# A list-scheduled opening for the first feed-forward stage of a decoder layer

## The chip, the cores and the metric

The kernel runs on one core of a Trainium2 chip. The metric is the device time of one execution in microseconds (us); the median of three runs is given. Five engines matter: TensorE (PE, matmuls; PEld is its weight load), VectorE (DVE), ScalarE (ACT), GpSimd (POOL) and SyncE (SP), which issues the DMAs.

## The reference

One decoder layer on 1,040 tokens (16 meta tokens and 1,024 of the sequence), width 1,024: a half-step SwiGLU, a mix of sparse and sliding-window attention, a second half-step SwiGLU, a last norm. What the change touches is the first SwiGLU:

```python
h = h + 0.5 * swiglu(rmsnorm(h, norm_ffn1[l]), w_ffn1_gate[l], w_ffn1_up[l], w_ffn1_down[l])

def rmsnorm(x, g):
    xf = x.astype(jnp.float32)
    y = xf * lax.rsqrt(jnp.mean(xf * xf, axis=-1, keepdims=True) + EPS)
    return (y * g.astype(jnp.float32)).astype(x.dtype)

def swiglu(x, w_gate, w_up, w_down):
    return (jax.nn.silu(x @ w_gate) * (x @ w_up)) @ w_down
```

with d_ff = 2816, all in float32. The attention stage between the two feed-forward stages is left as it is in code; the way in which it is ordered is touched (below).

## The kernel before

**Data.** Activations stand transposed: eight tiles `h[x][k]` of 128 features each, for two token halves x = 0 (528 columns, meta tokens among them) and x = 1 (512). A float32 operand is split into a high and a low float16 part; a product is three float16 matmuls (high by high, high by low, low by high, `mm3`, L438). Splitting is one ScalarE copy (high) and one VectorE subtraction (low): `split_w` (L421) for weights, `split_x` (L528) for activations.

**Feed-forward stage** (`ffn`, L521). The 22 blocks of d_ff go in pairs. From the second part on, a pair's gate or up weights are multiplied by a seven-product form of a 2 by 2 block product (`fast`, L711): combined weights (`sums`, L627) meet combined activation blocks t1 to t4 (tiles `tb`), and VectorE adds the seven results up as they leave the product banks pa, pb, pc and pd (`half_products`, L742, order `UP`, L730). Each such job is 168 matmuls, and while it runs the steps of the next job's weights (`prepare`, L672) and the splits of the finished hidden blocks (`split_later`, L831) are dealt out between its products by `pump` (L702).

**The opening.** The loads are issued in the order h[0], the identity, the gains, two weights, h[1]. The norm of half 0 (`norm_stats`, L460, `norm_bcast`, L478, `norm_u`, L502) squares on ScalarE and sums on VectorE; that of half 1 squares and sums on GpSimd (L927 to L931). `norm_stats` corrects the reciprocal root with four small VectorE steps. The first pair is multiplied plainly (`plain_pair`, L562): all of half 0 for gate, then `other_half()` (norm of half 1), then up, and half 1 after that. Before half 1's products the first combined weights (`wide_weights`, L650) and the combined blocks (`make_t`, L593) are ordered: twelve normed tiles are computed anew in float32 (`gained`, tiles `tu`), combined by four subtractions per block on GpSimd (`combine`, L584) and split. The normed tiles are not kept, but for four of half 1 (`saved`). All this runs in the order in which it is written.

**The planner.** The attention stage, with the last passes of the feed-forward stage ahead of it, isn't run as written: `Plan` (L136) records the instructions (`add`, L185), and `run` (L220) orders them by a list schedule with a cost for each (`cost`, L153). It takes, at each step, the engine that can go first and, there, the ready instruction recorded earliest. A tile in a product bank counts as one whole in its dependences (L83), a buffer is free when its last-recorded user is done (L242), and a VectorE instruction with two float32 inputs outside the banks is priced 0.4 us higher while GpSimd works (L214, L292). Each engine then runs its instructions in the order so found.

Of the kernel before, what the change touches and what calls it, by code (L numbers as in the profile page):

```python
# [46 lines left out]
class View:  # L47
# [34 lines left out]
    def box(self):  # L82
        if self.base.whole or not self.ops or not isinstance(self.ops[0], tuple):  # L83
            return None
        idx = self.ops[0][1]
        idx = [i for i in (idx if isinstance(idx, tuple) else (idx,)) if i is not None]
        res = []
        for i, n in zip(idx, self.base.shape):
            if isinstance(i, int):
                res.append((i % n, i % n + 1))  # L90
            elif isinstance(i, slice) and (i.step in (None, 1)):
                a, b, _ = i.indices(n)
                res.append((a, b))
            else:
                res.append((0, n))
        return res
# [9 lines left out]
class Lazy(View):  # L106
    def __init__(self, shape, dt, make, key, bufs, whole):
        View.__init__(self, self, (), shape, dt)
        self.make, self.key, self.bufs, self.whole = make, key, bufs, whole
        self.made = None  # L110
        self.live = False
        self.seen = []
        self.last = self.first = None
# [22 lines left out]
class Plan:  # L136
# [48 lines left out]
    def add(self, engine, op, args, kw):  # L185
# [34 lines left out]
    def run(self, keep=(), margin=0.25, early=0.0):  # L220
# [21 lines left out]
        for b in tiles.values():  # L242
            if id(b) not in kept and b.last is not None:
                dies[b.last].append(b)
# [30 lines left out]
        while len(order) < count:  # L275
# [51 lines left out]
        for b in tiles.values():  # L327
            b.seen, b.first, b.last = [], None, None
# [17 lines left out]
def layer_kernel(ctx: ExitStack, tc: tile.TileContext, xT, gains, wgu1, wd1, win, wvi, wbs, wbw, wout,  # L346
# [53 lines left out]
    ph["S"] = 2  # L400

    h = [[hp([P, HW[x]], F32, "h") for _ in range(KD)] for x in range(2)]

    def load_h(x):
        for k in range(KD):
            nc.sync.dma_start(h[x][k], xT[k][:, HS0[x]:HS0[x + 1]])

    load_h(0)
    ident = new(cst, [P, P], F32, name="ident")
    nc.sync.dma_start(ident, eye)  # L410
    g_all = new(cst, [P, 4, KD], F32, name="g_all")
    nc.sync.dma_start(g_all, gains)
# [47 lines left out]
    def norm_stats(acc, subs):  # L460
# [60 lines left out]
    def ffn(u, rb, hs, gi, wgu, wd, other_half, passes, saved, before_passes):  # L521
# [40 lines left out]
        def plain_pair(f):  # L562
            ws = [load_w(wgu[2 * f + i], 1024, raws.pop(0) if raws else None) for i in range(4)]
# [147 lines left out]
        def fast(weights, blocks, order):  # L711
# [5 lines left out]
                    "p53": ("pd", s4, b22, wb, wb, False)}  # L717
# [24 lines left out]
        def half_products(m, blocks, first, done):  # L742
            make = fbtmp if m else ftmp
            for what, ps in joint(blocks, UP):
# [17 lines left out]
                else:  # L762
                    c12 = va(base)[:, :, :wb]
                    nc.vector.tensor_add(c12, ps, c12)
                    done(1, base, c12)

# [72 lines left out]
        vals = plain_pair(0)  # L839
        blocks = (u[0][:4], u[0][4:], u[1][4:]) + tuple(t_blocks)  # L840
        with tc.manual_schedule(engines=ORDERED):
            for f0, f1 in F_GROUPS:
# [4 lines left out]
                for f in range(f0, f1, 2):  # L847
# [16 lines left out]
                    if f < NF - 2:  # L864
                        gates = gate_part(blocks)
# [46 lines left out]
    u1, rb1 = [], []  # L912

    def ffn1_norm(x):
        acc = new_acc() if x == 0 else acc_b
        for k in range(KD if x == 0 else 0):
            square_into(k, h[x][k], acc)
        u, rb = norm_u(norm_stats(acc, SUB_ALL[x]), h[x], 0, SUB_ALL[x], keep=True, saved=saved1 if x else None)
        u1.append(u)
        rb1.append(rb)  # L920

    saved1 = {}
    raws = [load_raw(wgu1[i], 1024) for i in range(2)]
    load_h(1)
    ffn1_norm(0)
    acc_b = new_acc()
    for k in range(KD):  # L927
        sq = acc_b if k == 0 else ftmp("sq")
        nc.gpsimd.tensor_mul(sq[:, :512], h[1][k], h[1][k])
        if k:  # L930
            nc.gpsimd.tensor_add(acc_b[:, :512], acc_b[:, :512], sq[:, :512])  # L931
# [8 lines left out]
    def to_mix():  # L940
# [4 lines left out]
    acc = ffn(u1, rb1, h, 0, wgu1, wd1, lambda: ffn1_norm(1),  # L945
              ((0, SUB_ALL[0], lambda r: mix_norm(0, r)), (1, SUB_ALL[1], None)), saved1, to_mix)
# [596 lines left out]
```

## Time and profile before

| | us |
|---|---|
| median of three runs | 2007.55 |
| lowest and highest | 2007.20, 2009.01 |
| the profiled execution, its own time | 2009.06 |
| its span, first to last instruction | 2007.3 |
| TensorE busy in the span | 1922.9 |
| VectorE busy | 1630.3 |
| ScalarE busy | 898.2 |
| GpSimd busy | 385.1 |

The first feed-forward stage takes up to about 640 us, the attention stage to about 1350, the second feed-forward stage the rest. Busy time is an average over stages with different limits; what one stage is worth is read from that stage. Neighbouring instructions of one engine can overlap a little, so that the distance between their starts is shorter than their durations.

### The profile page before, as it was taken

What the parts mean: (1) busy time and instruction counts of PE and PEld (TensorE: products, weight loads), DVE (VectorE), ACT (ScalarE), POOL (GpSimd) and SP (SyncE); (2) the same over time, 40 slices, a digit from 0 to 9 for tenths busy, and PEclk for the clock granted to TensorE, in tenths of its full rate; (3) what the DMA queues carried; (4) which work ended last, traced back from release to release, by engine and by line L of the source; (5) the groups of instructions that cost most, each with busy time, mean ns of one, the idle gap of its engine ahead of it and who ended that gap; (6) DMA issues with size and microseconds to landing.
All of it is one profiled execution on the core that took longest, in us unless ns stands there. A gap on an engine that the chain in (4) does not pass through costs nothing.

```text
span 2007.3 us, 32840 instructions
## 1 busy us (share of the span) xinstructions
PE 1922.9 (96%) x13080; PEld 1201.4 (60%) x13080; DVE 1630.3 (81%) x2787; ACT 898.2 (45%) x1602; POOL 385.1 (19%) x313
## 2 busy tenths in 40 slices
PE   5899999999998999999999999998899999999997
PEld 4588888888887655655555656444344444444443
DVE  7988778788774899999998977566987888788767
ACT  4434233333322455669887555434333333243232
POOL 4511312221220033131000000002322213312200
PEclk9899999999999999999999999999999999999998
DMA  4011111211121554221111231341112111211213
GB/s 160 11 54 58 59 64 38 69 64 59 48 85 38 190 160 149 69 91 64 32 48 43 85 102 52 105 147 42 43 38 68 63 58 48 64 63 48 79 37 131
DMA packets 58873, 146.95 MB, mean 73 GB/s; under 512 B 7264, under 2 KB 13408, under 8 KB 58720
## 3 DMA queue, kind: packets, MB, share of 16 engines
q1 hardware_dynamic: 58720, 144.86, 22.6%
q8 instruction: 102, 1.67, 0.3%
q14 instruction: 51, 0.42, 0.1%
HBM read 130.01 MB, written 14.76 MB: 72 GB/s over the span
## 4 chain that ended last, share of the span: by engine, by line
PE 79%; DVE 12%; ACT 5%; issue 2%; DMA 1%; POOL 1%; SPq 0%; DVEq 0%; ACTq 0%; POOLq 0%
PE pc L188 15%; PE pd L188 15%; PE pa L188 15%; PE pb L188 7%; PE p_gate L326 7%; PE p_out L326 4%; PE p_br L326 3%; PE pdn L188 2%; PE ptr L326 2%; PE rp L326 2%; ACT jk L326 1%; PE pdn L326 1%; PE pv_b L326 1%; DVE wsp L326 1%; DVE sc L326 1%
## 5 line engine op out<-in xcount | busy, mean ns | idle before, releaser
L188 PEld LDWEIGHTS <-wsp 128*128 128x128 f16 x4848 | 478.0, 99 | 293.2 <-issue 30.9
L188 PEld LDWEIGHTS <-x 128*128 128x128 f16 x3132 | 307.2, 98 | 156.5 <-issue 7.0
L326 PEld LDWEIGHTS <-wsp 128*128 128x128 f16 x2448 | 235.8, 99 | 223.0 <-issue 6.9
L188 PE MATMUL pa<-u,wsp 128*128 128x264 f16 (+1 forms) x1440 | 224.7, 310 | 0.0
L326 PE MATMUL p_gate<-u,wsp 128*128 128x512 f16 x768 | 188.4, 379 | 0.0
L188 POOL TENSOR_TENSOR h<-h,base 128x512 f32<-128x512 f32 (+1 forms) x72 | 116.3, 1615 | 291.1 <-DVE base L188 229.7
L326 PE MATMUL rp<-u,wsp 128*128 128x512 f16 (+2 forms) x624 | 140.2, 366 | 4.0 <-DVE rt L326 3.7
L188 ACT ACTIVATE wsp<-wst 128x1024 f16<-128x1024 f32 (+2 forms) x88 | 80.4, 915 | 142.3 <-DMA wst<-in_wd_dram 50.4
L326 DVE SCALAR_TENSOR_TENSOR wsp<-wst,wsp 128x1024 f16<-128x1024 f32 (+2 forms) x104 | 107.5, 1036 | 27.3 <-ACT wsp L326 27.0
L188 PE MATMUL pb<-tb,wsp 128*128 128x264 f16 (+1 forms) x720 | 114.0, 312 | 8.7 <-ACT tb L188 5.9
L188 PE MATMUL pc<-tb,x 128*128 128x264 f16 (+1 forms) x720 | 114.0, 313 | 5.1 <-DVE c L188 5.0
L326 ACT ACTIVATE wsp<-wst 128x1024 f16<-128x1024 f32 (+2 forms) x104 | 91.1, 880 | 58.4 <-PE p_out L326 16.4
L188 PE MATMUL pc<-tb,wsp 128*128 128x256 f16 (+1 forms) x720 | 113.6, 313 | 0.0
L188 PE MATMUL pd<-u,x 128*128 128x256 f16 (+1 forms) x720 | 110.7, 308 | 0.0
L188 PE MATMUL pd<-tb,x 128*128 128x256 f16 (+1 forms) x720 | 110.7, 308 | 0.0
L188 POOL TENSOR_TENSOR t<-g,g 128x512 f32<-128x512 f32 x16 | 25.5, 1592 | 434.4 <-DVE g L188 434.4
L188 ACT ACTIVATE wsp<-sa 128x1024 f16<-128x1024 f32 (+1 forms) x64 | 62.3, 973 | 101.4 <-DVE sa L188 101.2
L326 ACT ACTIVATE jk<-sc,s5nb 128x784 f16<-128x784 f32 (+2 forms) x93 | 98.1, 1055 | 15.9 <-DVE s5nb L326 13.1
L188 PE MATMUL pa<-hid,wsp 128*128 128x264 f16 (+1 forms) x648 | 103.1, 310 | 0.0
L188 PE MATMUL pd<-hid,x 128*128 128x256 f16 (+1 forms) x648 | 101.6, 308 | 0.0
L188 DVE TENSOR_TENSOR c<-pc,base 128x512 f32<-128x512 f32 x80 | 55.4, 692 | 55.1 <-PE pc L188 54.8
L188 ACT ACTIVATE base<-pa 128x528 f32<-128x528 f32 (+1 forms) x64 | 38.2, 598 | 133.6 <-PE pa L188 133.6
(218 smaller groups left out, 3494.7 us busy)
## 6 DMA issues: line engine op xcount, KB each, us to landing
wst<-in_wgu_dram SPq DMA_DIRECT2D x88, 512.0 KB, 3.8
wst<-in_win_dram SPq DMA_DIRECT2D x44, 512.0 KB, 3.5
wst<-in_wd_dram SPq DMA_DIRECT2D x48, 384.0 KB, 3.5
wst<-in_wd_dram SPq DMA_DIRECT2D x32, 256.0 KB, 2.8
wst<-in_wout_dram SPq DMA_DIRECT2D x16, 512.0 KB, 3.7
qscr<-ry SPq DMA_DIRECT2D x20, 256.0 KB, 2.1
q<-qscr SPq DMA_DIRECT2D x20, 256.0 KB, 3.1
wst<-in_wbs_dram SPq DMA_DIRECT2D x16, 256.0 KB, 3.2
```

The source lines that it names most:

```text
L188: return getattr(engine.real, op)(*[give(a) for a in args], **{k: give(v) for k, v in kw.items()})
L326: getattr(engine.real, op)(*[give(a) for a in args], **{k: give(v) for k, v in kw.items()})
```

## The change

The planner is switched on from the first line, and the whole opening, up to the end of the first seven-product gate part, is recorded and put in order by it (`nc.run` behind the first gate part). `first_pair` takes the place of `plain_pair` in this stage; the second feed-forward stage still uses `plain_pair`.

- Tokens go in three slices: columns 0 to 272 and 272 to 528 of half 0, and half 1. h[0] is loaded in two parts (`CUT`), the first one ahead of all else. All three slices square on ScalarE and sum on VectorE.
- The float32 normed tiles (`un`) are kept, so no `tu` tile is computed again. They take four of the 36 large tiles, all eight `late` tiles and four of the six `ft` tiles.
- The blocks are combined on VectorE. The hidden blocks are still combined on GpSimd.
- The first gate part has the order `FIRST`, with a separate product p3 in bank pb ahead of the rest, and seven VectorE evictions in place of five.
- The correction of the reciprocal root takes three steps (`newton`), in all norms.
- The planner's rules: product-bank tiles are compared by columns between matmuls, a buffer is free when all its users are done, all users of a new tile come behind its first, instructions with float16 inputs count as slowed by GpSimd too and per-partition scalars don't count, and the surcharge is 0.5. These hold for the attention stage as well.

```diff
-        if self.base.whole or not self.ops or not isinstance(self.ops[0], tuple):
+        if not self.ops or not isinstance(self.ops[0], tuple):
...
-                    if (write or wrote) and j != i and overlap(box, other):
+                    if (write or wrote) and j != i and (overlap(box, other) or b.whole and not (
+                            engine.name == "PE" == self.items[j][0].name)):
                         deps.add(j)
-                if write and box is None:
+                if write and (box is None or b.whole and engine.name != "PE"):
                     b.seen = []
...
-                b.last = i
-        shared = sum(v.dt == F32 and not v.base.whole for v in ins) > 1 and not any(v.base.whole for v in ins)
+                elif b.made is None and b.first != i:
+                    deps.add(b.first)
+                if b.uses[-1:] != [i]:
+                    b.uses.append(i)
+        shared = sum(v.shape[1:] != (1,) for v in ins) > 1 and not any(v.base.whole for v in ins)
...
-                busy, done = busy + 0.4, done + 0.4
+                busy, done = busy + 0.5, done + 0.5
...
-                if b.key in free:
-                    free[b.key].append(end + 0.1)
+                b.left, b.till = b.left - 1, max(b.till, end + 0.1)
+                if b.key in free and not b.left:
+                    free[b.key].append(b.till)
...
+    CUT = 272
+    for k in range(KD):
+        nc.sync.dma_start(h[0][k][:, :CUT], xT[k][:, :CUT])
...
-        nc.vector.tensor_mul(e[:, :nb], r[:, :nb], r[:, :nb])
-        nc.vector.tensor_mul(e[:, :nb], e[:, :nb], a[:, :nb])
-        nc.vector.tensor_scalar(e[:, :nb], e[:, :nb], -0.5, 1.5, op0=ALU.mult, op1=ALU.add)
-        nc.vector.tensor_mul(r[:, :nb], r[:, :nb], e[:, :nb])
+        newton(r[:, :nb], e[:, :nb], a[:, :nb])
...
+        def first_products(m, blocks, first, done):
+            for what, ps in joint(blocks, FIRST):
...
+                elif what == "p3":
+                    c12 = ftmp("c12")
+                    nc.scalar.activation(vb(c12), ps, AF.Copy)
...
+                elif what == "p5":
+                    nc.vector.tensor_add(vb(c22), ps, vb(c22))
+                    nc.vector.tensor_add(vb(c12), ps, vb(c12))
+                elif what == "p6":
+                    nc.vector.tensor_add(vb(c22), ps[:, :, :wb], vb(c22))
+                    done(3, c22, vb(c22))
+                    nc.vector.tensor_add(va(base), ps, va(base))
+                    nc.vector.tensor_add(vb(c12), va(base)[:, :, :wb], vb(c12))
+                    done(1, c12, vb(c12))
...
+            squares(0)
+            norm(0)
+            weight(0)
+            for k in range(KD):
+                norm_part(0, k)
+                if k in (1, 3, 5):
+                    weight((k + 1) // 2)
+                if k == 4:
+                    squares(1)
+            norm(1)
+            matmuls(0, tuple(range(KD)))
+            for k in range(KD):
+                norm_part(1, k)
+                if k == 2:
+                    squares(2)
+            norm(2)
+            matmuls(1, tuple(range(KD)))
...
+            for i in range(4):
+                t1 = ftmp("t1")
+                a1, b1, a2, b2 = un[0][i], un[1][i], un[0][i + 4], un[1][i + 4]
+                nc.vector.tensor_sub(vb(t1), vb(b1), va(a1)[:, :, :wb])
+                nc.vector.tensor_sub(vb(b1), vb(b2), vb(b1))
+                nc.vector.tensor_sub(va(a1)[:, :, :wb], vb(b2), vb(t1))
+                nc.vector.tensor_sub(va(a2), va(a2), va(a1))
...
+        FIRST = ("p1", "p3", "c11", "p7", "p5", "p6", "p74")
...
-                        gates = gate_part(blocks)
+                        gates = (parts.pop() if parts else gate_part)(blocks)
+                        if nc.on:
+                            nc.run(keep=hs[0] + hs[1] + u[0] + u[1][4:] + sum(t_blocks, []) + [ident, ones, g_all]
```

## Rows read from the trace of the kernel before

**Rows 1.** The page's forty slices of 50 us: busy tenths of TensorE.
```profile
PE   5899999999998999999999999998899999999997
```

**Rows 2.** Stretches: us, busy us of each engine (instructions), granted clock, DMA share, GB/s.
```profile
0.00:20.00 20.00, 4.80 (x20) 4.45 (x21) 10.27 (x18) 10.12 (x14) 7.05 (x10) 1.00 0.77 272
20.00:115.00 95.00, 74.24 (x476) 50.84 (x476) 87.43 (x115) 42.15 (x71) 44.79 (x30) 0.93 0.13 45
115.00:640.00 525.00, 522.90 (x4707) 460.26 (x4704) 403.63 (x512) 174.72 (x255) 110.13 (x68) 1.00 0.18 56
640.00:950.00 310.00, 289.93 (x2164) 179.54 (x2165) 286.67 (x714) 188.05 (x451) 70.52 (x68) 0.98 0.38 121
```

**Rows 3.** TensorE in order of time: start us, us, group, [idle before, its releaser].
```profile
11.40 2.29 PE L188 MATMUL nsum<-ones,acc 128*128 128x1 f32 x10 [11.40 <-DVE acc L188]
...
20.17 0.38 PE L188 MATMUL pg<-u,wsp 128*128 128x264 f16 x1 [0.20 <-ACT u L188]
...
51.69 2.05 PE L188 MATMUL nbc<-ident,n_r 128*128 128x128 f32 x8 [4.19 <-DVE n_r L188]
...
74.82 5.34 PE L188 MATMUL pg<-u,wsp 128*128 128x512 f16 x24
...
93.41 0.38 PE L188 MATMUL pb<-tb,wsp 128*128 128x264 f16 x2 [3.34 <-ACT tb L188]
...
107.66 4.53 PE L188 MATMUL pc<-tb,x 128*128 128x264 f16 x24 [2.73 <-DVE c L188]
...
114.65 2.86 PE L188 MATMUL pa<-u,wsp 128*128 128x264 f16 x24
117.35 2.86 PE L188 MATMUL pb<-tb,wsp 128*128 128x264 f16 x24
```

**Rows 4.** The chain that ended last, 0 to 140 us, by line.
```profile
by line: DVE u L188 10.3%; issue 8.9%; PE pc L188 7.9%; DVE tb L188 6.0%; PE pa L188 5.8%; POOL tu L188 5.7%; PE pd L188 5.6%; DVE un L188 5.1%; PE pb L188 3.9%; DVE wsp L188 3.7%; POOL t L188 3.6%; DMA h<-in_xT_dram 3.2%; PE pg L188 3.0%; 
```

**Rows 5.** VectorE by form, 0 to 107 us: count, busy us, mean ns, idle before.
```profile
L188 DVE TENSOR_TENSOR u<-un,u 128x512 f16<-128x512 f32 x8 | 9.7, 1265 | 0.0
```

**Rows 6.** GpSimd by form, 0 to 107 us.
```profile
L188 POOL TENSOR_TENSOR tu<-tu 128x528 f32<-128x528 f32 x4 | 6.8, 1694 | 0.2
```

**Rows 7.** VectorE in order of time while GpSimd idles, 66 to 76 us.
```profile
69.25 0.68 DVE L188 TENSOR_TENSOR tb<-t,tb 128x512 f16<-128x512 f32 x1
69.85 0.69 DVE L188 TENSOR_TENSOR tb<-tu,tb 128x528 f16<-128x528 f32 x1
70.47 0.68 DVE L188 TENSOR_TENSOR tb<-un,tb 128x512 f16<-128x512 f32 x1
...
73.51 1.21 DVE L188 SCALAR_TENSOR_TENSOR wsp<-wst,wsp 128x1024 f16<-128x1024 f32 x1
74.65 0.69 DVE L188 TENSOR_TENSOR tb<-tu,tb 128x528 f16<-128x528 f32 x1
```

**Rows 8.** VectorE in order of time, 0 to 54 us: norm steps and 256-wide instructions.
```profile
15.29 1.12 DVE L188 TENSOR_SCALAR n_e<-n_e 128x5 f32<-128x5 f32 x1
...
42.45 0.42 DVE L188 TENSOR_TENSOR u<-un,u 128x256 f16<-128x256 f32 x1
42.78 0.48 DVE L188 SCALAR_TENSOR_TENSOR un<-h,g_all,nbc 128x256 f32<-128x256 f32 x1
43.18 0.69 DVE L188 TENSOR_TENSOR sa<-wst 128x512 f32<-128x512 f32 x1
...
50.98 0.16 DVE L188 TENSOR_TENSOR n_e<-n_e,n_a 128x4 f32<-128x4 f32 x1
51.18 0.17 DVE L188 TENSOR_SCALAR n_e<-n_e 128x4 f32<-128x4 f32 x1
```

**Rows 9.** ScalarE in order of time, 0 to 24 us: first and last square of half 0.
```profile
3.54 0.64 ACT L188 ACTIVATE acc<-h 128x528 f32<-128x528 f32 x1 [1.53 <-DMA h<-in_xT_dram]
...
9.75 0.65 ACT L188 ACTIVATE sq<-h 128x528 f32<-128x528 f32 x1 [0.17 <-DVE acc L188]
```

**Rows 10.** SyncE in order of time: its first issues.
```profile
0.74 3.93 SPq L188 DMA_DIRECT2D h<-in_xT_dram  x8
```

More of the change, by code (lines that the diff above doesn't have):

```diff
@@ L112, in __init__ @@
         self.seen = []
-        self.last = self.first = None
+        self.first = None
+        self.uses, self.till = [], 0.0
     def real(self):
@@ L242, in run @@
         for b in tiles.values():
-            if id(b) not in kept and b.last is not None:
-                dies[b.last].append(b)
+            if id(b) not in kept:
+                b.left = len(b.uses)
+                for i in b.uses:
+                    dies[i].append(b)
         for q in queues.values():
@@ L327, in run @@
         for b in tiles.values():
-            b.seen, b.first, b.last = [], None, None
+            b.seen, b.first, b.uses, b.till = [], None, [], 0.0
         self.items, self.old = [], []
@@ L400, in layer_kernel @@
     ph["S"] = 2
+    nc.start()
     h = [[hp([P, HW[x]], F32, "h") for _ in range(KD)] for x in range(2)]
[L404 to L408, printed above, removed]
+    CUT = 272
+    for k in range(KD):
+        nc.sync.dma_start(h[0][k][:, :CUT], xT[k][:, :CUT])
+    g_all = new(cst, [P, 4, KD], F32, name="g_all")
+    nc.sync.dma_start(g_all, gains)
     ident = new(cst, [P, P], F32, name="ident")
     nc.sync.dma_start(ident, eye)
-    g_all = new(cst, [P, 4, KD], F32, name="g_all")
-    nc.sync.dma_start(g_all, gains)
     ones = new(cst, [P, 1], F32, name="ones")
@@ L562, in plain_pair @@
         def plain_pair(f):
-            ws = [load_w(wgu[2 * f + i], 1024, raws.pop(0) if raws else None) for i in range(4)]
+            ws = [load_w(wgu[2 * f + i], 1024) for i in range(4)]
             vals = [None] * 4
@@ L765, in half_products @@
                     done(1, base, c12)
+        def first_products(m, blocks, first, done):
+            for what, ps in joint(blocks, FIRST):
+                if what == "p1":
+                    base = fbtmp("base")
+                    nc.scalar.activation(va(base), ps, AF.Copy)
+                elif what == "p3":
+                    c12 = ftmp("c12")
+                    nc.scalar.activation(vb(c12), ps, AF.Copy)
+                elif what == "c11":
+                    first(ps)
+                elif what == "p7":
+                    c22 = ftmp("c22")
+                    nc.vector.tensor_add(vb(c22), ps, va(base)[:, :, :wb])
+                elif what == "p5":
[7 more added lines that the diff above has]
+                    done(1, c12, vb(c12))
+                else:
+                    c21 = ftmp("c21")
+                    nc.vector.tensor_add(va(c21), ps, va(base))
+                    done(2, c21, va(c21))
         def gate_part(blocks):
@@ new lines, in first_gate, with first, done @@
+        def first_gate(blocks):
+            gates = [None] * 4
+            def first(ps):
+                t = ftmp("g11")
+                nc.scalar.activation(va(t), ps, AF.Silu, scale=1.0 / WS)
+                gates[0] = (t, va(t))
+            def done(i, t, v):
+                nc.scalar.activation(v, v, AF.Silu, scale=1.0 / WS)
+                gates[i] = (t, v)
+            first_products(0, blocks, first, done)
+            return gates
+        FIRST = ("p1", "p3", "c11", "p7", "p5", "p6", "p74")
@@ L840, in ffn @@
+        parts = [gate_part]
+        if u is None:
+            vals, u, t_blocks = first_pair()
+            parts = [first_gate]
+        else:
+            vals = plain_pair(0)
         blocks = (u[0][:4], u[0][4:], u[1][4:]) + tuple(t_blocks)
@@ L864, in ffn @@
                     if f < NF - 2:
-                        gates = gate_part(blocks)
+                        gates = (parts.pop() if parts else gate_part)(blocks)
+                        if nc.on:
+                            nc.run(keep=hs[0] + hs[1] + u[0] + u[1][4:] + sum(t_blocks, []) + [ident, ones, g_all]
+                                   + [t for t, _ in gates] + [t for t, _ in weights[1]] + fetched[2]
+                                   + sum(down, []))
                 if not last:
@@ L910, in ffn @@
         return acc
[L912 to L926, printed above, removed]
-    for k in range(KD):
[L928 to L931, printed above, removed]
+    raws = [load_raw(wgu1[0], 1024)]
+    for k in range(KD):
+        nc.sync.dma_start(h[0][k][:, CUT:], xT[k][:, CUT:HS0[1]])
+    raws.append(load_raw(wgu1[1], 1024))
+    for i in (2, 3):
+        raws.append(new(ph["sb"], [P, 1024], F32, tag="wS", name="wst", bufs=2))
+        nc.sync.dma_start(raws[i], wgu1[i])
+    for k in range(KD):
+        nc.sync.dma_start(h[1][k], xT[k][:, HS0[1]:])
     u2 = []
```

95 lines of the change are left out of this document (91 added, 4 removed).

## Prediction

> **What bounds the kernel now.** I read the page's forty slices first [rows 1]: TensorE is at 9 tenths nearly everywhere, and the first two slices (100 us) stand out with 5 and 8. The table by stretch [rows 2] makes that a number. From 115 to 640 us, the rest of the first feed-forward stage, TensorE is busy 522.9 of 525 us: there it is the bound, and whatever arrives earlier at 115 us is passed on whole. From 20 to 115 us it is busy 74.2 of 95, and in the first 20 us 4.8. In the attention stage (640 to 950 us) it idles 20.1 us, and VectorE is busy 286.7 of 310. So the change has about 36 us to win in the opening, and a second place, the attention stage, which the same planner orders, where it can win or lose.
>
> Next, what ends last in the opening. VectorE is busy 87.4 of its 95 us there, and in the chain of waits of the first 140 us [rows 4] VectorE's lines (u, tb, un, wsp) and GpSimd's (tu, t) lead, beside queue time: TensorE waits for normed tiles and then for combined blocks. The TensorE row of times [rows 3] shows it: first matmul at 20.17 us, a wait for tb at 93.41, one for c at 107.66, and only from 114.65 on does a product follow a product without a gap.
>
> Why VectorE is late: its instructions are slow while GpSimd works. A 512-wide subtraction into u averages 1265 ns over eight [rows 5]. The same kind of instruction, with GpSimd idle, starts every 0.60 to 0.62 us [rows 7] (durations of 0.68 overlap, so I price by distance between starts). GpSimd takes about 1.69 us for one of its 528-wide subtractions [rows 6], and is busy 44.8 us between 20 and 115.
>
> **The change part by part.**
>
> *Prices on VectorE, GpSimd quiet:* 512 wide 0.61 us, 1024 wide 1.14 (73.51 to 74.65) [rows 7]; 256 wide 0.33 for a subtraction and 0.40 for a normed tile, mean 0.37 [rows 8], which I take for 272 too; a small instruction of the norm 0.20 [rows 8].
>
> *Start.* The first slice is 272 columns. The eight loads are still eight issues, 3.93 us in all [rows 10]. The first square began at 3.54, 2.8 us after the first issue [rows 9]; the eighth issue begins near 4.2, so its half-size tile is there near 7.0 and its square and sum are done near 7.8, against 11.40 for the first sum on TensorE now [rows 3]. Before, 8.8 us pass from that sum to the first matmul. Three blocks in place of five save about two fifths of the two groups of small matmuls, 1.9 us; the four small steps of the root's correction, one of which took 1.12 us while GpSimd squared [rows 8], become three of 0.2 because squaring leaves GpSimd, 2.4 us less. So 4.5 us: first matmul at 12.3, VectorE's stream from 11.5. The loads behind (weights, second half) come from the same queue in a new order; SyncE was not late for anything but the first tiles, and I cost the order at nothing, with 2 us if the second slice's tiles come after it is wanted. One new wait stands in that queue: the two loads for the first combined weights wait for staging tiles that the first splits free, with the next job's loads behind them; VectorE wants them 25 us later.
>
> *VectorE from 11.5 until the last combined block.* Sums of squares of slices two and three: 7 at 0.34 and 7 at 0.61, 6.6 (slice three's were GpSimd's; the squares themselves go to ScalarE, busy 42 of 95 us [rows 2], whose idle time hides them). Two norms of five steps, 2.0. Three weight splits, 3.4 (the first lies in the norm's wait). Normed tiles, two instructions each: 32 at 0.37 and 16 at 0.61, 21.6. Six gating products, 2.7. First combined weights: 7 at 0.61 and 2 at 1.14, 6.6. Combined blocks, 16 moved over from GpSimd, 9.8. Their low parts, 16, 9.8. The twelve recomputed normed tiles (tu) are gone. Sum 62.5, so 74.0.
>
> *VectorE in the first gate part.* Evictions 7 instead of 5 (new order, one more product bank): 4.3. Seven low parts of hid, 4.3. Weights of the next job, 5 at 0.61 and 3 at 1.14, 6.5. Together 15.1. GpSimd still combines hid: 4 instructions of 1.6 us, during which VectorE runs at half its rate, 3.2 more. So 92.3 us without a stall. Stalls: before, VectorE idled 7.6 us of 95; the list can fill some of that, but it prices a block of the norm's broadcast at 0.13 us where four took 2.05 [rows 3], and knows nothing of a slow TensorE clock. I take 5.5, bounds 0 and 15: 97.8.
>
> *TensorE.* 96 matmuls of 512 columns at 5.3 per 24 and 360 narrow ones at 2.70 per 24 (114.65 to 117.35) [rows 3] are 61.9 us, two more norms 5, a start at the low clock 3: it could finish the first gate part at 82.2. VectorE, not TensorE, is therefore the bound in the new opening, and the wait moves: not the first gate but the second product of the next part (bank pb) needs the last but one weight split of VectorE's list, done 1.1 us before its end, at 96.7. That product starts at 117.35 now [rows 3]: 20.6 us earlier. Against it, TensorE has then waited some 9 us; the granted clock of 20 to 115 us is 0.93 [rows 2], and after the wait at 107.66 a group of 24 took 4.53 us, where one at the upper level (2.4 GHz) takes 2.70 [rows 3]: 1.8 us back. Net 18.8, with 0 to 4 for the clock.
>
> *Combine on VectorE, the other way.* GpSimd would be busy 16 times 1.6, 26 us; with VectorE at half rate meanwhile it loses 13 us, more than the 9.8 it now pays. The Trainium skill (Perfetto Trace Analysis, Optimizing Scalar/DVE Operations) speaks against the move at first: from a saturated VectorE some work may go to ScalarE or even GpSimd, though it warns that GpSimd shares a read port with VectorE, so that it might not help. By the first half of that, keeping the blocks on GpSimd would end the opening 9.8 us sooner than my sum; by the measured 1265 against 610 ns, 3 us later.
>
> *Correction with three steps* in the other norms: 0.2 us each, twice or thrice on the path; 0.4 us less.
>
> *Planner.* Its rules for product banks, freed buffers and instructions slowed by GpSimd change for the attention stage too. No row shows that plan. The bounds are what stands there: its 20.1 us of TensorE idle [rows 2] can shrink or grow. VectorE has 23 us free in 310, so I take 0, with 4 either way.
>
> **The rivals.**
>
> *TensorE becomes the bound (A).* If the list hides all stalls and the hid work waits, VectorE ends at 89 to 92 and the pb product starts between 85 and 90: 27 to 32 us, a time near 1978. For it: VectorE had idle time that a list can fill. Against: 80.8 us of VectorE work after 11.5.
>
> *The list doesn't hold on the chip (B).* VectorE runs its plan in order; if TensorE's low clock delays a gating product that the plan put early, all behind it waits. Two or three waits as long as the 3.3 us one at 93.41 [rows 3] make 10 to 15 us of stalls: gain 8 to 11, near 1998.
>
> *Slower (C).* The new rules order the attention stage worse. Place: 640 to 950 us, where VectorE is at 92%. Price: each us that VectorE loses there, beyond its 23 us of slack, is one of the end. It decides from 23 us of added TensorE idle on, more than doubling the present 20.1; with 27 added the time is 2015.
>
> *No change (D).* The edit does what it says but its gain is lost: 15 to 22 us more idle in the attention stage, near 2007. That the opening itself gains nothing would need loads or buffers (36 large tiles, all taken) to hold back slice three by 20 us, and the 6.4 MB of input tiles and weights end near 24 us at the 272 GB/s of the first 20 us [rows 2].
>
> **How the numbers follow.** The sum is made against the profiled execution: 2009.06 us, span 2007.3, so 1.8 around it. The median of three runs is 2007.55, 1.5 below; the difference is taken off that. 18.8 and 0.4 give 19.2: 1988.4. The forecast's own range is 1983 to 1994. Chances: forecast 0.55, A 0.18, B 0.17, C 0.05, D 0.05. For 8 in 10 the range takes A and B in: 1976 (32 from the opening) to 1999 (8). A difference of 0.2% (4 us) is about what a measurement of this kernel tells from none. Faster: forecast, A and B, 0.90; same 0.05; slower 0.05.
>
> **What would show it.** Start: first matmul of bank pw near 12 us, first sum near 8. VectorE: 512-wide subtractions at 0.68 in the opening, GpSimd empty until the hid blocks. Bound: VectorE nearly full from 11 us to about 98, TensorE's last long wait ending at the second product of the next part, and no wait for tu or t. Hand-over: from there to the end of the stage TensorE idle stays near 2 us. Attention: its idle stays between 16 and 24. I am wrong if TensorE waits longest on a DMA, if VectorE shows gaps over 3 us behind a gating product, or if the attention stage differs by more than 4 us.

## The result and the profile after

| | before | after |
|---|---|---|
| median, us | 2007.46 | 1990.99 |
| lowest and highest | 2007.20, 2009.01 | 1989.84, 1993.28 |
| profiled span | 2007.3 | 1988.1 |
| first matmul of the first pair | 20.17 | 16.91 |
| pb product of the second part (the second product behind the first gate part, in bank pb) | 117.35 | 94.94 |
| last product of the first feed-forward stage | 634.5 | 612.1 |
| first matmul of the second feed-forward stage | 1360.1 | 1342.0 |

The ratio of the times is 0.9918 (95% interval 0.9901 to 0.9935). The forecast was 1988.4. In the traces, the opening gains 22.4 us (117.35 to 94.94 and still 634.5 to 612.1), the attention stage gives 4.3 back (725.6 us from the last product to the next stage's first matmul before, 729.9 after), and the second feed-forward stage differs by 1.1. That is 19.2 us between the two profiled spans, the forecast's number, but not from its terms. Between the medians it is 16.5: the profiled run of the changed kernel was the fastest of its four (1989.84), that of the kernel before (2009.06) as slow as the slowest of its.

The last two lines of the table are read from these rows of TensorE, before and then after:

```profile
634.50 2.78 PE L188 MATMUL pd<-u,x 128*128 128x256 f16 x24
...
1360.07 5.34 PE L188 MATMUL pg<-u,wsp 128*128 128x512 f16 x24 [0.78 <-DVE h L326]
```

```profile
612.10 2.78 PE L189 MATMUL pd<-u,x 128*128 128x256 f16 x24
...
1341.98 5.34 PE L189 MATMUL pg<-u,wsp 128*128 128x512 f16 x24 [0.78 <-DVE h L334]
```

The table by stretch of the changed kernel answers [rows 2] (busy us of TensorE, its weight loads, VectorE, ScalarE, GpSimd; then granted clock, DMA share, GB/s):

```profile
0.00:20.00 20.00, 4.94 (x20) 3.85 (x21) 10.48 (x26) 12.68 (x25) 0.20 (x4) 1.00 0.86 283
20.00:95.00 75.00, 70.23 (x499) 50.52 (x497) 71.63 (x130) 44.31 (x77) 12.66 (x4) 0.98 0.14 54
95.00:115.00 20.00, 20.00 (x182) 17.60 (x181) 17.47 (x24) 8.69 (x13) 2.32 (x2) 1.00 0.16 54
```

From 20 to 95 us TensorE is now busy 70.2 of 75 (before, 74.2 of the 95 us from 20 to 115), VectorE 71.6 of 75, GpSimd 12.7: TensorE and VectorE are nearly full at once.

TensorE in order of time, answering [rows 3] (start us, us, group, [idle before, its releaser]):

```profile
8.18 1.44 PE L334 MATMUL nsb<-ones,acc 128*128 128x1 f32 x6 [8.18 <-DVE acc L334]
...
16.91 0.61 PE L334 MATMUL pw<-u,wsp 128*128 128x272 f16 x2 [1.05 <-ACT u L334]
...
67.85 2.86 PE L334 MATMUL pa<-u,x 128*128 128x264 f16 x24
...
78.85 0.60 PE L334 MATMUL pc<-tb,wsp 128*128 128x256 f16 x4 [0.63 <-DVE tb L334]
...
81.90 2.86 PE L334 MATMUL pb<-tb,wsp 128*128 128x264 f16 x24
87.88 4.53 PE L334 MATMUL pc<-tb,x 128*128 128x264 f16 x24 [3.11 <-DVE c L334]
92.24 2.86 PE L189 MATMUL pa<-u,wsp 128*128 128x264 f16 x24
94.94 2.86 PE L189 MATMUL pb<-tb,wsp 128*128 128x264 f16 x24
```

There are two things to see. The first sum is ready at 8.18, but the first matmul comes 8.7 us later. And the last long wait, 3.11 us, stands inside the gate part, ahead of its last product (bank pc), not at the pb product, which follows without a gap.

Who holds the last product up is read from VectorE's order in those microseconds. The product needs bank pc emptied (c<-pc):

```profile
79.96 1.91 DVE L334 TENSOR_TENSOR hid<-silu,hid 128x528 f16<-128x528 f32 x3
81.80 0.68 DVE L334 TENSOR_TENSOR sb<-wst 128x512 f32<-128x512 f32 x1
82.40 0.68 DVE L334 TENSOR_TENSOR hid<-t,hid 128x512 f16<-128x512 f32 x1
83.00 0.68 DVE L334 TENSOR_TENSOR sa<-sb,wst 128x512 f32<-128x512 f32 x1
83.61 0.68 DVE L334 TENSOR_TENSOR hid<-silu,hid 128x512 f16<-128x512 f32 x1
84.21 0.68 DVE L334 TENSOR_TENSOR sa<-wst 128x512 f32<-128x512 f32 x1
84.81 0.68 DVE L334 TENSOR_TENSOR sb<-wst,sa 128x512 f32<-128x512 f32 x1
85.41 1.21 DVE L334 SCALAR_TENSOR_TENSOR wsp<-wst,wsp 128x1024 f16<-128x1024 f32 x1
86.55 0.68 DVE L334 SCALAR_TENSOR_TENSOR x<-wst,x 128x512 f16<-128x512 f32 x1
87.15 0.68 DVE L334 TENSOR_TENSOR c<-pc,base 128x512 f32<-128x512 f32 x1
```

The eviction stands behind eleven instructions, all recorded ahead of it: five splits of hidden blocks (hid), which nobody needs before the down projection, and six steps of the next weights (sb, sa, wsp, x). It starts 7.2 us after the first of them, though the product in bank pc (the row at 78.85) had ended by 79.5.

ScalarE's first instructions behind the squares show the late start:

```profile
10.45 1.06 ACT L334 ACTIVATE wsp<-wst 128x1024 f16<-128x1024 f32 x1 [2.86 <-DMA wst<-in_wgu_dram]
11.52 1.28 ACT L334 ACT_TABLE_LOAD   x1
12.82 0.20 ACT L334 ACTIVATE n_r<-n_a 128x3 f32<-128x3 f32 x1
```

The list put the first weight's split ahead of the norm's square root. On the chip ScalarE waits 2.86 us for that weight's transfer, with the root's table load and the root queued behind, though the sum was read at 9.66.

GpSimd, last, has one row unlike any before ([rows 6] has 1.69 us for a 528-wide subtraction, and no GpSimd instruction of the kernel before takes over 2.5):

```profile
71.17 1.60 POOL L334 TENSOR_TENSOR silu<-silu 128x512 f32<-128x512 f32 x1
80.80 7.57 POOL L334 TENSOR_TENSOR silu<-silu,t 128x512 f32<-128x512 f32 x1 [8.03 <-DVE hid L334]
```

### The profile page after: what moved, and what is told of

The parts are those of the page before. It is cut to its first block, busy times and chain, and to the rows that moved or that the text cites. A ratio compares the mean times of both kernels' runs of the same rounds, so it can differ in the third digit from the quotient of the medians.

```text
span 1988.1 us, 32868 instructions
## 1 busy us (share of the span) xinstructions
PE 1919.2 (97%) x13080; PEld 1197.5 (60%) x13080; DVE 1612.5 (81%) x2807; ACT 903.9 (45%) x1620; POOL 346.9 (17%) x282
## 4 chain that ended last, share of the span: by engine, by line
PE 73%; DVE 16%; ACT 6%; issue 3%; DMA 1%; SPq 0%; POOL 0%; DVEq 0%; ACTq 0%; POOLq 0%
PE pc L189 15%; PE pa L189 15%; PE pd L189 15%; PE pb L189 7%; PE p_gate L334 4%; PE p_out L334 4%; DVE sc L334 3%; PE p_br L334 2%; PE pdn L189 2%; ACT jk L334 2%; DVE wsp L334 2%; ACT psw L334 1%; PE pdn L334 1%; DVE m L334 1%; PE rp L334 1%
## 5 line engine op out<-in xcount | busy, mean ns | idle before, releaser
L189 PEld LDWEIGHTS <-x 128*128 128x128 f16 x3060 | 299.4, 98 | 151.9 <-issue 4.2
L189 PE MATMUL pa<-u,wsp 128*128 128x264 f16 (+1 forms) x1392 | 218.9, 312 | 0.0
L334 DVE SCALAR_TENSOR_TENSOR wsp<-wst,wsp 128x512 f16<-128x512 f32 (+2 forms) x109 | 114.0, 1049 | 29.2 <-ACT wsp L334 28.7
L189 ACT ACTIVATE wsp<-wst 128x1024 f16<-128x1024 f32 (+2 forms) x82 | 74.2, 905 | 138.0 <-DMA wst<-in_wgu_dram 50.7
L334 ACT ACTIVATE wsp<-wst 128x512 f16<-128x512 f32 (+2 forms) x109 | 96.1, 886 | 77.0 <-PE p_out L334 21.3
L189 PE MATMUL pc<-tb,x 128*128 128x264 f16 (+1 forms) x696 | 109.5, 311 | 2.6 <-DVE c L189 2.4
L189 PE MATMUL pc<-tb,wsp 128*128 128x256 f16 (+1 forms) x696 | 109.6, 312 | 0.0
L189 ACT ACTIVATE base<-pa 128x512 f32<-128x512 f32 (+1 forms) x63 | 37.7, 598 | 131.3 <-PE pa L189 131.3
L334 PE MATMUL p_br<-oT,wsp 128*128 128x512 f16 x384 | 96.6, 379 | 0.0
```

Of the source, the lines that this page charges most:

```text
L189: return getattr(engine.real, op)(*[give(a) for a in args], **{k: give(v) for k, v in kw.items()})
L334: getattr(engine.real, op)(*[give(a) for a in args], **{k: give(v) for k, v in kw.items()})
```

## The experiments

The theory, after this reading: (1) VectorE is the bound of the new opening; (2) its order and ScalarE's, not their sums, cost the 3.1 us wait and the late start; (3) the attention stage's loss comes from the planner's rules. Each experiment is compared by the start of the pb product of the second part (94.94) where it concerns the opening, since runs of one kernel scatter by 3 us as a whole, and by its median where it concerns the attention stage. e3 to e9 are one run each. Four profiled runs share the opening of the change (the changed kernel twice, e1 and e10); their pb product starts at 94.49 to 95.14, so that differences under 0.7 us say nothing.

### Which engine bounds the opening

e7 computes each combined block's low part twice.

```diff
                     split_x(tb[j][i], t[:, :WT[j]])
+                    nc.vector.tensor_sub(tb[j][i][:, 1, :], t[:, :WT[j]], tb[j][i][:, 0, :])
```

> The changed kernel, with the low part of each of the 16 combined blocks computed twice: 16 more VectorE instructions of 0.61 us, 9.8 us, in the opening. Theory (VectorE is the bound of the new opening): the second product of the next part (bank pb, 94.94 us after the change) starts 8 to 10 us later, the span is 1996 to 1998. Rival (TensorE is the bound there): under 3 us later, because VectorE's extra work lies beside matmuls.

```profile
96.92 4.79 PE L334 MATMUL pc<-tb,x 128*128 128x264 f16 x24 [7.75 <-DVE c L334]
101.55 2.86 PE L189 MATMUL pa<-u,wsp 128*128 128x264 f16 x24
104.25 2.86 PE L189 MATMUL pb<-tb,wsp 128*128 128x264 f16 x24
```

In TensorE's order of e7 the pb product starts at 104.25, 9.3 us later for 9.8 us of work (10.0 when both are counted from the first gate product, 67.12 against 67.85); the span is 1996.1. What is added to VectorE comes out at the end.

e8 adds to TensorE instead.

```diff
+                if name == "p1" and order is FIRST:
+                    for _ in range(3):
+                        product(ps, *w, tiles, stride, n, True, True)
                 product(ps, *w, tiles, stride, n, start, True)
```

> The changed kernel, with the first product p1 of the first gate part multiplied four times instead of once (only the last counts): 72 more matmuls, 8.1 us at 2.70 per 24. Theory (VectorE is the bound): they lie in waits for VectorE, of which the profile shows 3.1 us ahead of the last product and a slow group of 24 behind it, so the pb product of the next part starts at most 4 us later than 94.94. Rival (TensorE is the bound): 6 to 8 us later, span 1994 to 1996.

```profile
67.39 10.96 PE L334 MATMUL pa<-u,x 128*128 128x264 f16 x96
...
89.11 2.86 PE L334 MATMUL pb<-tb,wsp 128*128 128x264 f16 x24 [0.20 <-ACT c L334]
91.81 2.86 PE L334 MATMUL pc<-tb,x 128*128 128x264 f16 x24
...
97.21 2.86 PE L189 MATMUL pb<-tb,wsp 128*128 128x264 f16 x24
```

The pb product starts at 97.21: 8.1 us of matmuls cost 2.3. The first matmul also came 0.5 us earlier in e8 (16.43 against 16.91), so the matmuls themselves cost about 2.8. The other 5.3 or so lay in what VectorE's lateness had left open: 3.11 us of wait, 0.63 for tb, and some 1.7 for the 24 matmuls that ran at the lower clock after the wait (4.36 us from start to start against 2.70; the granted clock from 87.88 to 92.24 is 0.61). Both agree with the theory; with 5.3 us of slack TensorE is a near second. What the two show to be the bound is VectorE's queue as the list orders it, and not its sum of work: c2 (below) takes nothing off VectorE, only puts some instructions further back, and its gate part is 4.9 us shorter.

### Where the combination is done

e3 puts the 16 combinations back on GpSimd (`nc.vector.tensor_sub` to `nc.gpsimd.tensor_sub` in the four lines of the combination).

> The changed kernel with the 16 block combinations of the opening back on GpSimd. VectorE has 9.8 us less to do; GpSimd works some 26 us. Theory: what VectorE's other two-input instructions lose beside GpSimd, and the wait for GpSimd's slower results, is more; the pb product of the next part starts 2 to 8 us later than 94.94. Rival (take work off the fuller engine): it starts 3 to 9 us earlier. A third: GpSimd itself is held up while VectorE runs, as its one combination of 7.57 us at 80.8 suggests; then VectorE keeps 0.61 us apiece, GpSimd takes over 3 us apiece, and the start is over 8 us later.

The pb product starts at 97.29, 2.4 us later. VectorE's rows in e3 while GpSimd works:

```profile
64.17 1.76 DVE L334 TENSOR_TENSOR tb<-t,tb 128x512 f16<-128x512 f32 x1
65.86 5.17 DVE L334 TENSOR_TENSOR tb<-tu,tb 128x512 f16<-128x512 f32 x3
```

1.7 us apiece in place of 0.61. The 9.8 us saved are lost again, and 2.4 more, on the side of the first theory; the third (GpSimd held up over 3 us each) is out, since its sixteen took 1.60 to 1.73 us in the mean.

### The order of the first gate part

e5 takes the ordinary order (`parts = [first_gate]` left out).

> The changed kernel with the first gate part in the ordinary order (p1, p6, p7, p5, c11, p74, p53; five VectorE evictions instead of seven). Theory: the order of the change puts three products that need no combined block first, 8 us of matmuls that cover VectorE; without it TensorE waits for combined blocks from the second product on, and the pb product of the next part starts 2 to 6 us later than 94.94. Rival: the list takes whatever is ready in either order and two evictions of 0.61 are saved: within 1.5 us of 94.94, or earlier.

The pb product starts at 98.24, 3.3 us later. The wait ahead of the product that needs bank pc emptied grows from 3.11 to 5.88 us. The new order is worth about 3 us.

e4 gives the evictions precedence.

```diff
             for what, ps in joint(blocks, FIRST):
+                nc.shift = -4000
...
                     done(2, c21, va(c21))
+                nc.shift = 0
```

> The changed kernel, in the first gate part of which the evictions of the product banks are recorded ahead of all else that is ready, so VectorE takes them before the hidden blocks' low parts and the next job's weights. Theory: the wait of 3.1 us ahead of the last product (87.88, bank pc) and the slow 24 matmuls behind it go, 4.9 us; the next weights come later for it, so part of it returns as a wait at the pb product of the next part: that product starts 1 to 4 us earlier than 94.94. Rival: VectorE's sum decides alone, the wait only moves: 94 to 96.

It starts at 96.32, 1.4 us later: the rival's case, since 0.9 of it stands already at the first gate product (68.78 against 67.85), before the gate part that the experiment reorders; between 34 and 44.6 us TensorE's granted clock is 0.84 in this run and 1.00 in the changed kernel. The wait ahead of the last product is gone, but the first product of the next part then waits 3.76 us for its weight's low part (wsp), which now stands behind the evictions and hidden blocks:

```profile
92.62 3.91 PE L189 MATMUL pa<-u,wsp 128*128 128x264 f16 x20 [3.76 <-DVE wsp L334]
```

The evictions were not what had to be moved; the hidden blocks were (c2, below).

### The late root

e6 ties the first weight's split behind the square root, by an extra dependence in the list.

```diff
-        deps, new = set(), []
+        deps, new = set(self.also), []
...
+                rooted[s] = (len(nc.items),)
                 nc.scalar.activation(r, a, AF.Sqrt)
...
+            nc.also = rooted[0]
             weight(0)
+            nc.also = ()
```

> The changed kernel, with the first weight split tied behind the square root of the first slice's norm. In the changed kernel ScalarE waits 2.86 us for that weight's transfer with the root queued behind it: the sum is read at 9.66, the root comes at 12.82. Theory: the root comes near 10.0, the first matmul (16.91) 2 to 3 us earlier, and the pb product of the next part 2 to 3 us earlier than 94.94, since both engines are full from there. Rival: the time is lost later to another wait and the product stays within 1 us.

ScalarE in e6:

```profile
7.89 1.28 ACT L334 ACT_TABLE_LOAD   x1
10.42 0.20 ACT L334 ACTIVATE n_r<-n_a 128x3 f32<-128x3 f32 x1 [1.25 <-DVE n_a L334]
```

The table load falls into idle time and the root comes 2.4 us earlier. The first matmul comes at 14.81, 2.1 us earlier, and the pb product at 92.24, 2.7 us earlier. The span of e6's profiled run, 1988.7, does not show it; its attention and second feed-forward stages were 1.0 and 2.3 us longer than in the profiled run of the changed kernel, at the same order of instructions.

### How much is the list

e9 issues the opening in the order in which it is written, with the same instructions on the same engines (`order = list(range(count))` in `run`, for that part).

> The changed kernel with its opening issued in the order in which it is written instead of the list's. Same instructions, same engines. Theory: the gain is half the list's: VectorE then stands behind the slices' matmuls (each gating product waits for a whole slice of TensorE), and the pb product of the next part starts 15 to 30 us later than 94.94, at or behind the old kernel's 117.35. Rival: what was moved (no GpSimd beside VectorE, kept tiles, smaller first slice) is the gain, and the order costs under 8 us.

2050.19 us, and the pb product at 156.05: 61 us later than with the list and 39 behind the kernel before. The direction was expected, the size not. VectorE in e9:

```profile
12.81 0.50 DVE L336 SCALAR_TENSOR_TENSOR tu<-h,g_all,nsb 128x272 f32<-128x272 f32 x1 [0.33 <-PE nsb L336]
13.81 0.44 DVE L336 TENSOR_TENSOR u<-tu,u 128x272 f16<-128x272 f32 x1 [0.49 <-ACT u L336]
14.17 0.49 DVE L336 SCALAR_TENSOR_TENSOR tu<-h,g_all,nsb 128x272 f32<-128x272 f32 x1
```

Each normed tile waits 0.49 us for ScalarE's copy in the middle of it, and each gating product for a whole slice of matmuls (one wait of 14.13 us). Between 20 and 155 us VectorE is busy 81 of 135 us. In this written order the work that was moved brings nothing. Another written order was not tried, nor was the opening of the kernel before under the list, so that the 22.4 us are not shared out between the list and the work that was moved.

### The attention stage

e2 is the kernel before with only the new planner rules (class `View` to class `Plan` of the changed kernel).

> The kernel before with nothing but the new planner rules, so its opening is the old one and only the attention stage is planned anew. Theory: the stretch from the last product of the first feed-forward stage to the first matmul of the second goes from 725.6 to about 730, the span from 2007.3 to about 2011.5, and the two parts of the change add up. Rival: 725 to 726 and 2007, the rules alone cost nothing.

Its median is 2012.83 against 2008.70 beside it, a ratio of 1.0020 (1.0010 to 1.0029); the stretch from the last product to the second stage takes 730.0 us. The rules alone cost 4 us, and the two parts of the change add up: e10 (below), with the new opening and the order of before in the attention stage, lies 22.2 us under the kernel before.

e1 takes the rules back in the changed kernel.

```diff
+OLD = [False]
...
-        if not self.ops or not isinstance(self.ops[0], tuple):
+        if OLD[0] and self.base.whole or not self.ops or not isinstance(self.ops[0], tuple):
...
         open_phase("mix")
+        OLD[0] = True
         nc.start()
```

(and so for the dependence, buffer and surcharge rules.)

> The changed kernel, but the attention stage is planned by the rules of before (product banks as wholes, a buffer free at its last-recorded user, surcharge 0.4 by float32 inputs). The stretch from the last product of the first feed-forward stage to the first matmul of the second took 725.6 us before (634.5 to 1360.1) and 729.9 after (612.1 to 1342.0). Theory: the new rules cost these 4.3 us; the stretch falls to 725 to 727 and the span to about 1984. Rival: the loss has another cause (the stage begins at another moment, its loads meet other transfers); the stretch stays at 729 to 731, the span at 1988.

It doesn't decide between the two: 1989.51 in the median, from 1987.51 to 1992.34, and 731.2 us for the stretch in its profiled run, which was its slowest. Its list is not that of before: the shorter root correction, one instruction less in each of three norms of that stretch, was enough to order TensorE, ScalarE and VectorE differently.

e10 takes that correction back there too, so that TensorE, VectorE, ScalarE and GpSimd run this stretch in the order of the kernel before (by the names in the two traces).

> The changed kernel with the attention stage planned by the rules of before and with the four-step root correction there, so that from the attention stage on every engine's order is that of the kernel before; e1 still differed, since the shorter correction alone moved its list. Theory: the new plan costs about 4 us (e2: 2012.83 against 2008.70); the stretch returns to 725 to 727, the median lies 3 to 5 us under that of the changed kernel beside it, near 1986. Rival: the loss comes with the earlier start of the stage, whatever the plan: under 1.5 us between the two medians.

The changed kernel was run again beside it:

> The changed kernel once more, beside the next two on the same chip, to see how far its runs scatter. Its stretch from the last product of the first feed-forward stage to the first matmul of the second was 729.9 us; six kernels that share its attention plan (expectations e2 to e8) have 728.6 to 730.9 in one look each. Expected: opening unchanged (pb product at 94 to 96), median 1989 to 1992.

The six kernels are e3 to e8; e2 has an order of its own there.

The median of e10 is 1985.51 (1984.35 to 1987.47; ratio to before 0.9888, 0.9873 to 0.9902), that of the changed kernel beside it 1991.13 (1990.02 to 1992.60; 0.9915). The stretch is 724.2 us in e10, 730.0 in the changed kernel beside it:

```profile
611.65 2.78 PE L192 MATMUL pd<-u,x 128*128 128x256 f16 x24
...
1335.86 5.34 PE L192 MATMUL pg<-u,wsp 128*128 128x512 f16 x24 [0.78 <-DVE h L341]
```

So the new plan, rules and shorter correction together, costs 5.6 us there.

Where in the stage: TensorE waits about as much in both (23.4 us in e10, 24.4 in the changed kernel) and is busy 4.8 us longer. Its groups of small matmuls take longer. First e10, then the changed kernel run beside it, from the views that group TensorE's instructions over that stretch (count, busy us, mean ns):

```profile
L341 PE MATMUL ptr<-ident,psp 128*128 128x128 f32 x288 | 51.7, 282 | 0.2
...
L341 PE MATMUL pv_b<-vt,ptb 128*128 128x64 f16 x864 | 48.2, 193 | 0.6 <-ACT ptb L341 0.3
```

```profile
L334 PE MATMUL ptr<-ident,psp 128*128 128x128 f32 x288 | 54.1, 285 | 0.9 <-DVE oT L334 0.4 <-DVE ptb L334 0.2
...
L334 PE MATMUL pv_b<-vt,ptb 128*128 128x64 f16 x864 | 51.1, 193 | 0.4
```

The same 288 transposes and 864 narrow products cover 2.4 and 2.9 us more, while their mean durations hardly differ: they overlap less with their neighbours. The new rules let such matmuls of one bank pass each other, so this fits the rule for product banks. It goes with the rules and not with the correction: e2, with the new rules and the old correction, has 54.3 and 50.8 us for the two groups, e1, with the rules of before and the new correction, 51.6 and 48.0. But the rule for product banks alone was not tried, and which of the rules it is stays open. Nor was it enough to take the rules back: in e1 the groups are short, but TensorE waits 27.9 us in the stretch, 4.5 more than in e10, and it is as long as with the new rules. What e10 and c2 have and the others lack is the very order of before: 724.2 to 725.6 us by that order, 728.6 to 731.2 by the three others that ran.

### A faster version

c2 has e10's plan, e6's root, and the hidden blocks' splits last in the first gate part's list.

```diff
+        def late(step):
+            nc.shift = 4000 if nc.on else 0
+            step()
+            nc.shift = 0
...
-            when.append((0, lambda: nc.scalar.activation(dst[:, 0, :], t[:, :n], AF.Copy)))
-            when.append((0.7, lambda: nc.vector.tensor_sub(dst[:, 1, :], t[:, :n], dst[:, 0, :])))
+            when.append((0, lambda: late(lambda: nc.scalar.activation(dst[:, 0, :], t[:, :n], AF.Copy))))
+            when.append((0.7, lambda: late(lambda: nc.vector.tensor_sub(dst[:, 1, :], t[:, :n], dst[:, 0, :]))))
```

> As e10, with two mends of the opening: the first weight's split waits behind the first norm's root (e6, 2.7 us earlier at the pb product), and in the first gate part the splits of the hidden blocks come last in the list, so that evictions and the next weights are not queued behind them. Theory: the 3.1 us wait ahead of the last product and the slow 24 matmuls behind it (1.8 us) go too; the pb product of the next part starts at 87 to 89 instead of 94.94, and the median is 6 to 8 us under that of e10, near 1979. Rival: the hidden blocks' splits, now ahead of the next part's evictions, hold those up instead; only e6's 2.7 us are left.

```profile
79.14 2.86 PE L341 MATMUL pb<-tb,wsp 128*128 128x264 f16 x24
82.08 2.86 PE L341 MATMUL pc<-tb,x 128*128 128x264 f16 x24
84.77 2.86 PE L192 MATMUL pa<-u,wsp 128*128 128x264 f16 x24
87.47 2.86 PE L192 MATMUL pb<-tb,wsp 128*128 128x264 f16 x24
```

VectorE's eviction of bank pc, at 87.15 in the changed kernel, now starts ahead of all hidden blocks:

```profile
81.35 0.68 DVE L341 TENSOR_TENSOR c<-pc,base 128x512 f32<-128x512 f32 x1
```

TensorE in c2 goes through the end of the gate part with no wait of note, at the upper clock (2.69 us from 82.08 to 84.77; the granted clock from 20 to 95 us is 1.00). The pb product starts at 87.47, 7.5 us earlier than in the changed kernel: 2.6 of it stand at the first gate product (65.26 against 67.85), by the earlier root, and 4.9 come behind it, by the new place of the hidden blocks. Some of that returns: a wait of 0.44 us stands at 98.72, and the first stage's last product comes 6.5 us earlier (605.6 against 612.1), not 7.5. The median is 1980.10 (1979.38 to 1981.58; ratio to before 0.9861, 0.9845 to 0.9878): 5.4 us under e10 where 6 to 8 were expected, and 11.0 under the change.

## Why the prediction came out right, point by point

**The sum came near because two errors oppose each other.** It said 18.8 us from the opening, 0.4 from the correction and 0 from the attention stage. The runs show 22.4 from the opening and a loss of 4.3 to 5.6 behind it, and the median lies 2.6 us over the forecast. That the two errors nearly cancel is luck. The 0.4 is shown by no run; under the rules of before (e1) the shorter correction came with a longer stretch.

**Start.** The first slice's sum was to be ready at 7.8 and is at 8.18. But the 4.5 us from there to the first matmul are 8.7. The step that failed is the one that costed the loads' order at nothing: not SyncE but ScalarE was held by a load, with the root behind it. From the sum's reading (9.66) to the root (12.82) pass 3.2 us, where the kernel before takes 0.2 (13.73 to 13.93). The prediction had asked what is queued behind a waiting load, but on SyncE alone. e6 gives 2.7 us of it back at the pb product. Another 1.0 us had been taken off for a shorter broadcast and didn't come: the first normed tile starts 1.69 us after the broadcast's first matmul with five blocks (17.46 to 19.15, before) and with three (14.21 to 15.90).

**VectorE's sum.** From the first normed tile (15.90) to the last low part of a combined block (80.0) are 64.1 us; the sum had 62.5, with the squares of slice two in it, some of which lie earlier. The prices by distance between starts held: 0.60 for 512 wide, 1.14 for 1024. The whole list was to end at 97.8, 86.3 us after the stream's start, 80.8 without a stall; its last instruction ends at 97.5, 81.6 us after it. Most of the stall term of 5.5 was not needed: the list keeps VectorE busy 71.6 of 75 us.

**TensorE's sum.** It had 69.9 us from the first matmul to the end of the gate part (12.3 to 82.2); c2, where TensorE hardly waits, takes 69.9 (14.88 to 84.77). Its 3 us for a start at the low clock are not shown as such: from 16.9 to 27 us the granted clock of the changed kernel is 1.00, though the first 48 matmuls behind 18.76 start every 0.165 us and the next 43 every 0.116, which is 2.4 us; why stays open. Its "some 9 us" of waiting are 11.8 by its own numbers (96.7 less 82.2 and 2.7 for the product between), which changed nothing in the forecast.

**GpSimd beside it.** 3.2 us were reckoned; three VectorE instructions beside it took 1.16, 1.75 and 1.24 us, 2.1 in all over the 0.68 that they take alone. GpSimd paid instead: its 7.57 us.

**The bound, and where the wait goes.** That VectorE and not TensorE is the bound in the changed kernel is shown by e7 and e8; rival A (TensorE) is out there, but with only some 5.3 us to spare. c2 is rival A come true by hand, by A's own condition that the hidden blocks wait: pb product at 87.47, in its 85 to 90, and 1980.10 (with the order of before in the attention stage, so without the loss there) beside its 1978. The place of the last wait was wrong: not the pb product of the next part but the last product of the gate part, by an eviction queued behind instructions that nobody waits for yet. The prediction summed VectorE's work and didn't ask in which order it stands. The clock term was right in size: 24 matmuls in 4.53 us after the wait, as at 107.66 before [rows 3], though after a wait of 3.11 us and not of 9.

**The combination on VectorE.** 3 us later on GpSimd was the estimate, by the doubled price of VectorE's instructions; e3 measured 2.4. The Trainium skill's sentence on offloading from a full VectorE (Perfetto Trace Analysis, Optimizing Scalar/DVE Operations) would not have helped here. Its caution that between VectorE and GpSimd it might not help would have, and the trace agrees: beside GpSimd VectorE's instructions took 1.7 us in place of 0.61 in e3. That a shared port is the reason is shown by no run.

**The list on the chip (rival B).** Its mechanism did occur, once, at the root, for some 2.7 us and not 10 to 15, and on ScalarE rather than VectorE. Its price was also added up wrong: stalls of 10 to 15 us in place of 5.5 leave a gain of 9 to 14 us, not 8 to 11.

**The planner in the attention stage.** 0 within 4 was taken from the idle time there. The loss is 4.3 in the profile and 5.6 between medians, outside the bound, and it hardly shows as idle time: TensorE's idle time in the stretch is 23.8 us before and 24.4 after, its busy time 701.6 and 705.3. Rival C was right that the stage is ordered worse, at a quarter of its price, but not in how: the view that was read for it, TensorE's idle time, was the wrong one. The rest, 1.1 us in the second feed-forward stage, is within what single profiled runs differ by (645.5 to 648.4 us).

## What to carry to other kernels

When a step is put under a list schedule, price the bound engine by the distance between its starts, and then read the order, not only the sum: an instruction that releases another engine may stand behind some that nobody needs yet, and pushing those back paid where pulling the eviction forward didn't. Look for the first transfer that a queue has to wait for and at what is queued behind it, on every engine. And a planner that serves two stages has to be judged in both: here the new plan of the second gave back a quarter of what the first had won.

## What the runs showed that was not expected

GpSimd can be the one that loses. In the changed kernel its 512-wide combination at 80.80 took 7.57 us, until 88.4, while VectorE ran two-input instructions every 0.60 us and paused at 87.8 (in e3, which has the same order there, it took 7.57 again). The same one in c2 took 1.61, and there two of VectorE's two-input instructions, beside it and the GpSimd instruction behind it, took 1.18 and 1.78 where they take 0.68 or 0.69 alone. So either engine can be the one that loses; what decides it is not shown.

The length of a wait alone doesn't tell whether TensorE falls to its lower clock. After 3.11 us of wait (the changed kernel) 24 matmuls took 4.36 us from start to start at a granted clock of 0.61, after 7.75 (e7) 4.63 at 0.57; in e3, after waits of 3.65 and 2.88, the groups behind took 2.70 and 2.69 at 1.00.

One instruction less in each of three norms reorders the whole list of the attention stage, some 725 us long: e1 and e10 differ in it by that alone, and the stretch takes 731.2 and 724.2 us in their profiled runs. The ratios to before, 0.9903 (0.9888 to 0.9918) and 0.9888 (0.9873 to 0.9902), overlap, since e1's own runs scatter by 4.8 us.
